# Delta-rule stage of a hybrid encoder layer: the remainder of weight pieces by a negated rounding and an adding DMA

## The chip, the cores and the metric

One core of one Trainium2 chip runs the whole program. The metric is the device time of one execution in microseconds. The engines are TensorE (PE; PEld is its weight load, which overlaps), VectorE (DVE), ScalarE (ACT), GpSimd (POOL) and SyncE (SP, which issues DMAs). Each engine works through its own instructions in order; semaphores join the engines.

## The reference

One encoder layer over 640 tokens (512 of a prompt, 8 x 16 of a decoding group), model width 2048, all in fp32. Cut to its core:

```
z = x @ w_in                     # one projection: attention, delta-rule and gate columns
y_a = (fox_attend(q_a, k_a, v_a, forget) * silu(gate_a)) @ w_out_fox
qkv = silu(causal_conv4(qkv_b)); q, k = l2_normalize(q), l2_normalize(k)
o_b, state = gated_delta_chunked(q, k, v, g, beta, state0)
y_b = (rms_norm(o_b) * silu(gate_b)) @ w_out_gdn
h = (sigmoid(m_a) * y_a + sigmoid(m_b) * y_b) @ w_out
x1 = layer_norm(alpha * x + h)
out = x1 + sigmoid(x1 @ w_pl_gate) * rms_norm(p @ w_pl_proj)
```

The keys, values, forget logits, the convolution's last rows and the delta-rule states are outputs too.

## The kernel before

**Products in three parts.** An fp32 product is made of fp32r ("rounded") operands: a weight w is split into wh, its rounded value, and wl = w - wh, an operand x likewise into xh and xl. TensorE adds wh·xh, wh·xl and wl·xh. The 640 tokens are cut into two halves of 320, so one step of 128 weight rows takes six matmuls of 320 columns (`mm6`, called from `column`, L380 and L381). A column of 128 outputs has 16 such steps.

**From memory to a piece.** The weights come as halves of 128 x 1024 into `wr`, three buffers, by SyncE's DMA (L266, 512 KB). A half is cut into two pieces of 512 columns, each of which serves four steps. For each piece `w_piece` issues two instructions: ScalarE casts it to `wh` (L326), and VectorE subtracts, `wl` = `wr` - `wh` (L327). `wh` and `wl` have five buffers each (`PIECES`), so a new piece may overwrite a buffer when TensorE has used the piece made five earlier. `w_ahead` is called once in each step, ahead of its matmuls; it may issue one load and make one piece, if fewer than five are outstanding.

**Stages.** The front and the attention fill the time to about 900 us. In the delta-rule stage (about 945 to 1645 us, `phase_gdn`) the columns are those of q, k, v and gate for eight heads, and merge-gate columns that fill in between. Then come the output projections and the tail. For a part of the later columns sums of weights are prepared on GpSimd (`weight_sums`, L292, tile `ws`) and kept in memory (`wsums`).

**Lanes.** Between the steps of a column `tick` (L124) lets generators ("lanes") issue their next small step: the convolution (`strip`, L836 to L843, and `conv_silu` with `tails`, L849), the block work of a head (L978 on), the chunks (`gdn_chunks`, L998; `gdn_dec`, L1052) and the heads' ends (L1022 to L1042). At the start of `gdn_chunks` GpSimd copies `kpad`, `gpad` (L1003) and `uu` (L1008); six ticks later the first decode matmuls (L1060) read `kpad`. In `gdn_dec` GpSimd makes `vm` from ScalarE's `vnd` (L1069, L1072). In the recurrence over tokens ScalarE makes `vn` (L1162) from one small matmul for the next (L1165). The last head's normalised output is transposed by TensorE (L1037, L1041), multiplied on VectorE and split (L354, L355) as operand 15 of the columns that follow.

**What sets the order.** The program writes the order of every engine out by itself. `saw` adds an estimated duration for each instruction to a clock for its engine (VectorE 0.17 us + 0.0011 per element of a row, ScalarE 0.21 + 0.00085, GpSimd 0.25 + 0.0020), and a lane's next step is issued once the estimated result is due. So an instruction that goes to another engine moves the lanes' steps against the columns. Within one queue nothing is passed.

Of the kernel before, what the change touches and what calls it, by code (L numbers as in the profile page):

```python
# [9 lines left out]
F32 = mybir.dt.float32  # L10
# [4 lines left out]
ALU = mybir.AluOpType  # L15
# [37 lines left out]
class Kernel:  # L53
# [143 lines left out]
    def plan(self):  # L197

        n = self.i["w"].shape[0] // 2
        self.ops, self.halves, c = [], [], 0
        self.short = range(n - 48 + self.PLAIN, n - 40)
        self.wsums, self.later = {}, [*self.short, *range(n - 32, n - 16, 2), *range(n - 16 + self.GATES, n, 2)]
        while c < n:
            if c in self.short:

                for x in ("S2", "b"):
                    self.wsums[c, x] = self.tc.dram_tile([P, 1024], F32, name=f"ws{c}{x}")
                for i, (x, p) in zip((0, 1, 4, 3, 2, 6, 5), ((0, 0), ("S2", 0), ("S2", 1), ("b", 0), (0, 1), ("b", 1), (1, 1))):  # L210
                    if p == 0 or x == 1:
                        self.halves.append((c, x, "wr", 1 if x == 1 else 2))
                    self.ops.append(("p", (c, x), p, ((c, i), 0)))
                c += 1
                continue
            if c in self.later:

                for x in ("S1", "S2", "b", "S3"):
                    self.wsums[c, x] = self.tc.dram_tile([P, 1024], F32, name=f"ws{c}{x}")
                for i, key in enumerate(((c, 0), (c, "S2"), (c, 1), (c, "b"), (c, "S1"), (c + 1, 1), (c, "S3"))):  # L220
                    self.halves.append((*key, "wr", 2))
                    self.ops += [("p", key, p, ((c, i), p)) for p in range(2)]
                c += 2
                continue
            if self.PAIR0 <= c < self.PAIR0 + self.PAIRS * 2:
                self.halves += [(c, 0, "wr", 4), (c + 1, 0, "wr", 4), (c + 1, 1, "sr", 3), (c, 1, "wr", 3)]
                o = [("p", (c, 0), 0),
                     ("s", (c, "S1"), (c + 1, 0), (c + 1, 1), ALU.add),
                     ("s", (c, "S2"), (c, "S1"), (c, 0), ALU.subtract),
                     ("p", (c, "S2"), 1),  # L230
                     ("s", (c + 1, 0), (c, 0), (c + 1, 0), ALU.subtract),
                     ("p", (c, 1), 2),
                     ("s", (c, "S2"), (c, 1), (c, "S2"), ALU.subtract),
                     ("p", (c + 1, 0), 3), ("p", (c, "S1"), 4), ("p", (c + 1, 1), 5), ("p", (c, "S2"), 6)]
                for x in o:
                    if x[0] == "s":
                        self.ops.append(x)
                    else:
                        self.ops += [("p", x[1], p, ((c, x[2]), p)) for p in range(2)]
                c += 2  # L240
                continue
            cs = range(c, c + (2 if c == 0 else 1))
            for p in range(4):
                for x in cs:
                    if p % 2 == 0:
                        self.halves.append((x, p // 2, "wr", 2))
                    self.ops.append(("p", (x, p // 2), p % 2, (x, p)))
            c += len(cs)
        self.raw, self.wq, self.used = {}, {}, 0
        self.rest = 0  # L250
        self.nh = self.no = self.np = 0

    def w_new(self, tag):
        pool = self.wp if tag == "wr" else self.zp
        return pool.tile([P, 1024], F32, tag=tag, name=tag, bufs=3)
# [62 lines left out]
    def w_piece(self):  # L318
        nc = self.nc
        _, key, p, to = self.ops[self.no]  # L320
        self.no += 1
        self.np += 1
        src = self.w_use(key)[:, p * 512:p * 512 + 512]
        hi = self.wp.tile([P, 512], F32R, tag="wh", name="wh", bufs=self.PIECES)
        lo = self.wp.tile([P, 512], F32R, tag="wl", name="wl", bufs=self.PIECES)
        nc.scalar.copy(out=hi, in_=src)  # L326
        nc.vector.tensor_tensor(out=lo, in0=src, in1=hi.bitcast(F32), op=ALU.subtract)  # L327
        self.wq[to] = (hi, lo)

    def w_ahead(self):  # L330

        if self.nh < len(self.halves) and self.now >= self.rest and self.w_free(self.halves[self.nh][2]):
            self.w_load()
        if self.no == len(self.ops):
            return
        o = self.ops[self.no]
        if o[0] == "s":
            if o[2] in self.raw and o[3] in self.raw and (o[1] in self.raw or self.w_free("sr")):
                self.no += 1
                self.w_sum(*o[1:])  # L340
        elif self.np - self.used < self.PIECES and o[1] in self.raw:
            self.w_piece()
# [90 lines left out]
    def pair(self, xf, fin, each=None, uv=None, half=False):  # L433
# [32 lines left out]
        def add(out, a, b):  # L466
            nc.vector.tensor_tensor(out=out, in0=a, in1=b, op=ALU.add)
        nc.scalar.copy(out=u, in_=run(0, "X11", "a"))
        w = body(u)
        add(w, w, run(1, "T2", "b"))  # L470
        if half:
            add(v, w, run(4, "T1", "c"))
# [712 lines left out]
    def run(self, ctx):  # L1185
        nc, tc = self.nc, self.tc
        nc.push_inst_callback(self.saw)
        ctx.callback(nc.pop_inst_callback)
        self.cst = ctx.enter_context(tc.tile_pool(name="cst", bufs=1))
        self.xp = ctx.enter_context(tc.tile_pool(name="xp", bufs=KT))  # L1190
        self.wp = ctx.enter_context(tc.tile_pool(name="wp", bufs=2))
        self.ps = ctx.enter_context(tc.tile_pool(name="ps", bufs=4, space=bass.MemoryType.PSUM))
        dr = tc.dram_tile
        self.ogd = [dr([P, T], F32, name=f"ogd{i}") for i in range(16)]
        self.md = [dr([P, T], F32, name=f"md{i}") for i in range(32)]
        self.ed = [dr([P, T], F32, name=f"ed{i}") for i in range(16)]
        self.ld = dr([5, 4, 32, 32], F32, name="ld")
        self.xd = dr([80, 256], F32, name="xd")
        self.sqd = dr([P, T], F32, name="sqd")
        self.es = [dr([P, T], F32, name=f"es{i}") for i in range(16)]  # L1200
        self.rr = [dr([P, T], F32, name=f"rr{i}") for i in range(16)]
        self.sgd = [dr([P, T], F32, name=f"sgd{i}") for i in range(H)]
        self.sgf = [dr([P, T], F32, name=f"sgf{i}") for i in range(H)]
        self.qkd = {(h, i): dr([P, T], F32, name=f"qkd{h}{i}") for h in (0, *self.APART) for i in range(2)}
        self.vd = dr([5, P, 1024], F32, name="vd")
        self.kc, self.vc, self.bias = {}, {}, {}
        self.plan()
        self.col = 0
        self.op = [None] * KT
        self.cut = slice(0, HALF), slice(HALF, T)  # L1210
        self.nm = 0
        work, conv, self.ends = self.lane(), self.lane(True), self.lane()
        self.blocks, self.chunks, self.sums = self.lane(True), self.lane(), self.lane(True)
        self.work = work
        with tc.manual_schedule():
            with tc.tile_pool(name="ps2f", bufs=3, space=bass.MemoryType.PSUM) as self.ps2:
                with tc.tile_pool(name="zs", bufs=1) as self.zp:
                    self.front(work)
                with tc.tile_pool(name="zf", bufs=1) as self.zp:
                    self.phase_fox(work)  # L1220
            with tc.tile_pool(name="ps2g", bufs=4, space=bass.MemoryType.PSUM) as self.ps2, \
                    tc.tile_pool(name="cs2", bufs=1) as c2, tc.tile_pool(name="zg", bufs=1) as self.zp:
                self.cvst = c2.tile([P, 24, 24], F32, name="cvst")
                nc.sync.dma_start(out=self.cvst, in_=self.i["conv"])
                self.tails = c2.tile([P, 24, 27], F32, name="tails")
                self.nbanks = 4
                self.phase_gdn(conv, work)
            with tc.tile_pool(name="ps2b", bufs=4, space=bass.MemoryType.PSUM) as self.ps2, \
                    tc.tile_pool(name="zb", bufs=1) as self.zp:
                self.tail()  # L1230
# [1211 lines left out]
```

## Time and profile before

| | us |
|---|---|
| median of 3 runs | 2189.33 (2188.91 to 2189.61) |
| span of the profiled execution | 2185.3 |
| outside the span (median less span) | 4.0 |
| PE busy in the span | 2168.4 (99%) |
| DVE busy | 1555.4 (71%) |
| ACT busy | 924.8 (42%) |
| POOL busy | 317.7 (15%) |
| casts to `wh` (L326), whole span | 638, 389.9 |
| subtractions to `wl` (L327), whole span | 638, 442.4 |

The profiled execution has no time of its own beside its span: what lies around the span is taken from the runs' median. Columns of a stretch ("windows") are explained where they are shown. In a group "x176 | 123.2, 701 | 112.0 <-ACT wh L326 110.3" says 176 instructions, 123.2 us busy, 701 ns each, and 112.0 us of idle time of their engine just before them, of which 110.3 were ended by ScalarE's `wh`. In a list of waits the three numbers are us in total, times, and the longest.

### The profile page before, as it was taken

How to read it: one execution, taken by the hardware profiler on the slowest of the kernel's cores; microseconds unless marked ns; L12 is line 12 of the kernel's file. 1: busy time of each engine (PE TensorE's matmuls, PEld its weight loads, DVE VectorE, ACT ScalarE, POOL GpSimd, SP SyncE). 2: the span in 40 equal slices, each digit the busy share in tenths (PEclk: the TensorE clock that was granted, in tenths of full speed). 3: DMA queues.
4: the chain of work that ended last, by engine and by line, in shares of the span. 5: the costliest groups of instructions: out<-in, count | busy, mean ns of one | idle time of the engine just before them, and what ended most of it. 6: DMA issues, size and time to landing. Idle time of an engine off the chain costs nothing. (4 is left out here: it accounts for less than half of the span.)

```text
span 2185.3 us, 41804 instructions
## 1 busy us (share of the span) xinstructions
PE 2168.4 (99%) x15606; PEld 2101.9 (96%) x15606; DVE 1555.4 (71%) x3194; ACT 924.8 (42%) x2058; POOL 317.7 (15%) x542
## 2 busy tenths in 40 slices
PE   9999999999999999999999999999999999999998
PEld 7799999999999999999999999999999999999998
DVE  6877677667455456676776867767757787789987
ACT  4344444444333345334434535435434343354544
POOL 0022323333111101111121211210000000011100
PEclk9999999999999999999999999999999999999999
DMA  6356665666888857844535444436567656673475
GB/s 233 104 183 198 201 190 185 196 198 212 319 293 282 303 190 246 289 115 132 151 115 148 133 117 145 135 116 190 174 213 256 220 168 205 195 270 137 149 229 172
DMA packets 222283, 421.12 MB, mean 193 GB/s; under 512 B 33768, under 2 KB 118840, under 8 KB 222080
## 3 DMA queue, kind: packets, MB, share of 16 engines
q1 hardware_dynamic: 222080, 418.45, 58.9%
q8 instruction: 123, 2.02, 0.4%
q14 instruction: 80, 0.66, 0.1%
HBM read 323.29 MB, written 95.07 MB: 191 GB/s over the span
## 5 line engine op out<-in xcount | busy, mean ns | idle before, releaser
L327 DVE TENSOR_TENSOR wl<-wr,wh 128x512 fp32r<-128x512 f32 x638 | 442.4, 703 | 287.6 <-ACT wh L326 281.4
L326 ACT CAST wh<-wr 128x512 fp32r<-128x512 f32 x638 | 389.9, 618 | 317.8 <-PE g L381 137.7
L380 PE MATMUL g<-xh,wh 128*128 128x320 f32 (+1 forms) x1184 | 385.1, 325 | 0.2 <-ACT xh L354 0.2
L380 PE MATMUL g<-xl,wh 128*128 128x320 f32 (+1 forms) x1184 | 366.0, 309 | 0.3 <-DVE xl L355 0.3
L381 PE MATMUL g<-xh,wh 128*128 128x320 f32 x1184 | 366.0, 309 | 0.0
L381 PE MATMUL g<-xl,wh 128*128 128x320 f32 x1184 | 365.7, 309 | 0.0
L380 PE MATMUL g<-xh,wl 128*128 128x320 f32 (+1 forms) x1184 | 365.7, 309 | 0.0
L381 PE MATMUL g<-xh,wl 128*128 128x320 f32 x1184 | 365.5, 309 | 0.0
L458 PE MATMUL g<-xh,wh 128*128 128x320 f32 (+1 forms) x1072 | 334.0, 312 | 2.3 <-ACT m L1241 1.6
L458 PE MATMUL g<-xl,wh 128*128 128x320 f32 (+1 forms) x1072 | 332.0, 310 | 0.6 <-DVE xl L355 0.6
L458 PE MATMUL g<-xh,wl 128*128 128x320 f32 (+1 forms) x1072 | 332.0, 310 | 0.0
L292 POOL TENSOR_TENSOR ws<-ws 128x171 f32<-128x171 f32 (+2 forms) x184 | 135.5, 736 | 771.9 <-DMA ws<-in_w 763.3
L380 PEld LDWEIGHTS g<-xh,wh 128*128 128x128 f32 x1184 | 223.0, 188 | 12.3 <-issue 8.0
L381 PEld LDWEIGHTS g<-xh,wh 128*128 128x128 f32 x1184 | 223.1, 188 | 0.9
L380 PEld LDWEIGHTS g<-xl,wh 128*128 128x128 f32 x1184 | 222.8, 188 | 0.9 <-DVE xl L355 0.9
L380 PEld LDWEIGHTS g<-xh,wl 128*128 128x128 f32 x1184 | 222.4, 188 | 0.2 <-DVE wl L327 0.2
L381 PEld LDWEIGHTS g<-xl,wh 128*128 128x128 f32 x1184 | 222.6, 188 | 0.0
L381 PEld LDWEIGHTS g<-xh,wl 128*128 128x128 f32 x1184 | 222.3, 188 | 0.0
L458 PE MATMUL g<-t,wh 128*128 128x320 f32 (+1 forms) x976 | 216.6, 310 | 0.0
L458 PEld LDWEIGHTS g<-xh,wh 128*128 128x128 f32 x1072 | 201.8, 188 | 4.1 <-ACT m L1241 2.1
L458 PEld LDWEIGHTS g<-xl,wh 128*128 128x128 f32 x1072 | 201.6, 188 | 1.2 <-DVE xl L355 1.1
L458 PEld LDWEIGHTS g<-xh,wl 128*128 128x128 f32 x1072 | 201.9, 188 | 0.0
(443 smaller groups left out, 3594.4 us busy)
## 6 DMA issues: line engine op xcount, KB each, us to landing
wr<-in_w SPq DMA_DIRECT2D x259, 512.0 KB, 4.1
kc<-in_kc SPq DMA_DIRECT2D x32, 512.0 KB, 6.4
vc<-in_vc SPq DMA_DIRECT2D x32, 512.0 KB, 6.9
ws<-in_w SPq DMA_DIRECT2D x96, 128.0 KB, 3.5
md<-m SPq DMA_DIRECT2D x32, 320.0 KB, 3.3
t<-md SPq DMA_DIRECT2D x32, 320.0 KB
sr<-in_w SPq DMA_DIRECT2D x18, 512.0 KB, 3.6
ws<-in_w SPq DMA_DIRECT2D x100, 85.5 KB, 2.5
```

The costliest lines, as they stand in the source:

```text
L292: nc.gpsimd.tensor_tensor(out=o, in0=x, in1=y, op=op)
L326: nc.scalar.copy(out=hi, in_=src)
L327: nc.vector.tensor_tensor(out=lo, in0=src, in1=hi.bitcast(F32), op=ALU.subtract)
L380: nc.tensor.matmul(ps[0], whl[w], xhl[o][:, a], start=(first and x == 0), stop=(last and x == 2))
L381: nc.tensor.matmul(ps[1], whl[w], xhl[o][:, b], start=(first and x == 0), stop=(last and x == 2))
L458: nc.tensor.matmul(ps, a[:, w], b, start=(k == 0 and n == 0 and not more), stop=(k == last and n == 2), skip_group_check=True)
```

## The change

For pieces that are made after the start of the delta-rule stage, of columns that are neither prepared sums nor among the last 48, the remainder is made in another way: ScalarE writes `lo` = -(the weights), which the fp32r tile rounds, so -wh; then a DMA on GpSimd's queue reads the same piece of the weights from memory and adds it to `lo` in place. The DMA is not issued in `w_piece`, but by `w_adds` in the first `w_ahead` that is at least one tick later. 160 of the 638 pieces are made so: all that belong to delta-rule heads and to merge gates in the stage.

```diff
--- before.py
+++ after.py
@@ -249,6 +249,8 @@
         self.raw, self.wq, self.used = {}, {}, 0
         self.rest = 0
         self.nh = self.no = self.np = 0
+        self.summed, self.adds = False, deque()
+        self.SUMMED = n - 48
 
     def w_new(self, tag):
         pool = self.wp if tag == "wr" else self.zp
@@ -324,11 +326,23 @@
         hi = self.wp.tile([P, 512], F32R, tag="wh", name="wh", bufs=self.PIECES)
         lo = self.wp.tile([P, 512], F32R, tag="wl", name="wl", bufs=self.PIECES)
         nc.scalar.copy(out=hi, in_=src)
-        nc.vector.tensor_tensor(out=lo, in0=src, in1=hi.bitcast(F32), op=ALU.subtract)
+        c, hf = key
+        if self.summed and key not in self.wsums and c < self.SUMMED:
+            nc.scalar.mul(lo, src, -1.0)
+            self.adds.append((self.now + 1, lo, self.i["w"][2 * c + hf][:, p * 512:p * 512 + 512]))
+        else:
+            nc.vector.tensor_tensor(out=lo, in0=src, in1=hi.bitcast(F32), op=ALU.subtract)
         self.wq[to] = (hi, lo)
 
+    def w_adds(self):
+
+        while self.adds and self.adds[0][0] <= self.now:
+            _, lo, src = self.adds.popleft()
+            self.nc.gpsimd.dma_start(out=lo, in_=src, accum_op=ALU.add)
+
     def w_ahead(self):
 
+        self.w_adds()
         if self.nh < len(self.halves) and self.now >= self.rest and self.w_free(self.halves[self.nh][2]):
             self.w_load()
         if self.no == len(self.ops):
@@ -1224,6 +1238,7 @@
                 nc.sync.dma_start(out=self.cvst, in_=self.i["conv"])
                 self.tails = c2.tile([P, 24, 27], F32, name="tails")
                 self.nbanks = 4
+                self.summed = True
                 self.phase_gdn(conv, work)
             with tc.tile_pool(name="ps2b", bufs=4, space=bass.MemoryType.PSUM) as self.ps2, \
                     tc.tile_pool(name="zb", bufs=1) as self.zp:
```

In the whole program this takes 160 instructions from VectorE (L327), adds 160 to ScalarE (L331) and 160 DMAs to GpSimd (L341, 256 KB each; GpSimd issued none before). SyncE's DMAs stay the same in number, and so do TensorE's matmuls: 13152 of the main stream (fp32r) and 1388 small ones (fp32). Their order changes: TensorE's row order passes 507 times from main matmuls to small ones or back before, 489 times now, so it leaves the main stream 9 times less. The planner counts the new instructions, and lane steps of the stage stand between 160 main matmuls earlier and 72 later than before. Outside the stage the order is the same. Lines shift: L326 is L328, the subtraction L334, and what stands behind is 14 lines further down (L1003 is L1017, L1037 is L1051).

On GpSimd's queue, at the start of a head's chunks in the middle of the stage; `ws` are the weight sums, `kpad`, `gpad` and `uu` the copies for the decode matmuls, `vm` the masked `vnd`. Before:

```order
L292 TENSOR_TENSOR ws<-ws 128x171 x8
L1003 COPY kpad<-kq_9936 128x4x16 x2
L1003 COPY gpad<-gr 128x4x16 x2
L1008 COPY uu<-u_11695 32x5x32 x4
L292 TENSOR_TENSOR ws<-ws 128x171 x4
L838 MEMSET strip 128x3
L843 COPY strip<-cvst 128x8x3
L849 COPY tails<-strip 128x3
L850 COPY tails<-strip 128x24
L1072 TENSOR_TENSOR vm<-vnd,cb 128x256
```

With the change:

```order
L341 DMA wl<-in_w 128x512 x5
L294 TENSOR_TENSOR ws<-ws 128x171 x4
L341 DMA wl<-in_w 128x512
L1017 COPY kpad<-kq_9936 128x4x16 x2
L1017 COPY gpad<-gr 128x4x16 x2
L1022 COPY uu<-u_11564 32x5x32 x4
L341 DMA wl<-in_w 128x512 x3
L1086 TENSOR_TENSOR vm<-vnd,cb 128x256
L341 DMA wl<-in_w 128x512
```

Adds (L341) now stand right in front of and behind the copies, and `vm` has three ahead of it and one behind.

On ScalarE's queue, around the convolution's copies out of PSUM in the same stage. Before:

```order
L1069 ACTIVATE vnd<-s,cs 128x128
L839 COPY strip<-g 128x320
L840 COPY strip<-g 128x192
L842 COPY strip<-g 128x8x16
L326 CAST wh<-wr 128x512
L854 ACTIVATE cy<-strip,taps 128x664
L1081 COPY ob<-s 128x128
L326 CAST wh<-wr 128x512
L1162 ACTIVATE vn<-s,cs 128x128
```

With the change:

```order
L328 CAST wh<-wr 128x512
L331 ACTIVATE wl<-wr 128x512
L853 COPY strip<-g 128x320
L854 COPY strip<-g 128x192
L856 COPY strip<-g 128x8x16
L328 CAST wh<-wr 128x512
L331 ACTIVATE wl<-wr 128x512
L868 ACTIVATE cy<-strip,taps 128x664
L1176 ACTIVATE vn<-s,cs 128x128
```

Each cast is followed by the scaling of the same piece (L331), which the lanes' own steps now have in front of them.

On TensorE's queue, at the last head's output transposes. Before, with 30 main matmuls (L458) between them and the first column of the next stage (L380):

```order
L458 MATMUL g<-xl,wh 128x320
L458 MATMUL g<-xh,wl 128x320
L1037 MATMUL s<-cb,ob 128x128 x4
L1041 MATMUL s<-cb,ob 128x128
L458 MATMUL g<-xh,wh 128x320
```

With the change:

```order
L472 MATMUL g<-xl,wh 128x320
L472 MATMUL g<-xh,wl 128x320
L1051 MATMUL s<-cb,ob 128x128 x4
L1055 MATMUL s<-cb,ob 128x128
L394 MATMUL g<-xh,wh 128x320
L395 MATMUL g<-xh,wh 128x320
```

The transposes have moved behind those 30 matmuls and stand directly ahead of the next stage's column.

## The prediction

> **What bounds the kernel now.** First the busy times by stretch (window; length; busy us and instructions of PE, PEld, DVE, ACT, POOL; granted clock; DMA share; GB/s). The change acts in the delta-rule stage, 945 to 1645 us.
>
> ```profile
> 945.00:1645.00 700.00, 697.86 (x5281) 673.69 (x5280) 500.53 (x1400) 303.78 (x843) 102.51 (x246) 1.00 0.49 147
> 300.00:400.00 100.00, 100.00 (x683) 100.00 (x683) 71.41 (x93) 40.65 (x77) 33.12 (x31) 1.00 0.59 189
> 546.00:765.00 219.00, 217.03 (x1840) 201.81 (x1840) 110.63 (x262) 77.28 (x195) 26.53 (x46) 1.00 0.86 299
> ```
>
> TensorE is idle for 700 − 697.86 = 2.14 us of the stage, at full clock. VectorE, which the change relieves, is busy 72% of it, ScalarE 43%, GpSimd 15%. The second row is a stretch of nothing but main matmuls: 100/683 = 0.1464 us each. Next, what TensorE waited for in the whole span (us in total, times, longest):
>
> ```profile
> PE g L458 <- ACT m L1241: 1.6, 1, 1.6
> ...
> PE s L1152 <- DVE S L1170: 1.2, 1, 1.2
> ...
> PE s L1165 <- ACT vn L1162: 0.8, 1, 0.8
> ...
> PE g L458 <- DVE wl L327: 0.2, 1, 0.2
> ```
>
> The subtraction that the change takes away (`wl`, L327) held TensorE up once in 2185 us, for 0.2 us. The 1.2 and the 0.8 are nearly all that was lost in the stage. So VectorE is no bound: the gain to be had is 2.14 us, plus whatever the new order saves in TensorE's own work. 0.2% of the time, about what a measurement can tell from no change, is 4.4 us.
>
> **The change part by part.** The groups of the stage (count | busy, mean ns | idle before, by releaser):
>
> ```profile
> L327 DVE TENSOR_TENSOR wl<-wr,wh 128x512 fp32r<-128x512 f32 x176 | 123.2, 701 | 112.0 <-ACT wh L326 110.3 <-DMA out_stp<-S 1.1
> L326 ACT CAST wh<-wr 128x512 fp32r<-128x512 f32 x177 | 109.9, 621 | 86.7 <-PE g L381 68.4 <-DMA wr<-in_w 10.4 <-PE g L458 3.2
> L292 POOL TENSOR_TENSOR ws<-ws 128x171 f32<-128x171 f32 x80 | 49.9, 624 | 101.6 <-DMA ws<-in_w 97.0
> L1008 POOL COPY uu<-u 32x160 f32<-32x160 f32 x32 | 12.4, 387 | 136.7 <-DMA u<-xd 80.8 <-PE g L381 54.9
> L1003 POOL COPY kpad<-kq 128x64 f32<-128x64 f32 x16 | 5.3, 359 | 0.0
> ```
>
> *Off VectorE:* 160 subtractions × 0.70 = 112 us, 500 to 389 of 700. Hidden before, so worth nothing by itself.
>
> *Onto ScalarE:* 160 scalings of the same 128x512 piece. No such instruction is in the trace; the cast L326, same engine and shape, takes 0.62, so +99 us, 304 to 403 of 700 (58%). It lies beside TensorE. What it may cost is lane steps (the delta rule's small matmuls) that wait behind a scaling on ScalarE's queue: nothing at the least, and at the most 0.62 in front of each of the four `vn` (L1162) of eight heads, 32 × 0.62 = 20 us. The program's planner counts ScalarE's time and sets those steps later, and in the whole stage ScalarE's `vn` cost 0.8; I take +0.7, that row once more.
>
> *Onto GpSimd:* 160 issues of an adding DMA, 256 KB each. GpSimd issued none before; the rows for an issue are SyncE's (min/median/max in ns of the weight loads, L266) and what these loads and others took to land:
>
> ```profile
> L266 SPq DMA_DIRECT2D wr<-in_w x82: 327/333/1519, 946.4 to 1644.5; - x82
> ...
> DMA to landing us min/median/max: 3.4/3.7/5.0
> ```
>
> ```profile
> wr<-in_w SPq DMA_DIRECT2D x259, 512.0 KB, 4.1
> ...
> ws<-in_w SPq DMA_DIRECT2D x100, 85.5 KB, 2.5
> ...
> es<-ed SPq DMA_DIRECT2D x16, 320.0 KB, 8.1
> ```
>
> An issue costs 0.33 to 1.5 us by these; I take 1.0, since GpSimd needs 0.36 even to copy 64 elements (L1003) where the bigger engines' cheapest work takes less. GpSimd goes from 102.5 to about 262 of 700. Landing: at least the 2.5 of an 85 KB load; at most 16.2, twice the slowest row, since an adding DMA reads its destination too. I take 4.1, the whole span's median for 512 KB: that is as many bytes as 256 KB read twice over, and the stage's DMA load moves towards the span's.
>
> Whether this is hidden is a budget. A piece is 24 matmuls, 24 × 0.1464 = 3.51 us; with five buffers a piece released is first needed after the four others, 14.06 us later, more where lane work stands between. One such release before, ScalarE and VectorE, with the last number the idle time ahead:
>
> ```profile
> 960.43 0.62 ACT L326 CAST wh<-wr 128x512 fp32r<-128x512 f32 x1 [2.90 <-PE g L381]
> ```
>
> ```profile
> 961.08 0.69 DVE L327 TENSOR_TENSOR wl<-wr,wh 128x512 fp32r<-128x512 f32 x1 [2.03 <-ACT wh L326]
> ```
>
> Before: cast and subtraction, 1.34 us of 14.06. Now: cast 0.62 + scaling 0.62 + up to four weight sums ahead on GpSimd 4 × 0.62 = 2.5 + issue 1.0 + landing 4.1 = 8.8. That leaves 5.2 us; cost nothing. If the cover is gone the price is steep: everything beyond 14.06 is shared out over five buffers, 0.2 us a piece for each us too late.
>
> *Waits added:* each add waits on GpSimd's queue for ScalarE's scaling (and for the add five pieces earlier, long landed). GpSimd used to run ahead; now it cannot pass TensorE's releases. Behind an add stand, at the start of each head, the copies `kpad`, `gpad` and `uu`, on which decode matmuls depend. They take 4 × 0.36 + 4 × 0.39 = 3.0 us and are issued six steps ahead, 6 × 6 × 0.1464 = 5.3 us: with one add of 1.0 in front 1.3 us are over; two take 0.3 of it back. I take 0 here; the rivals have the rest.
>
> *SyncE:* 160 subtractions no longer hold the raw weight buffer, but the scaling does, which ends as early (961.05 + 0.62 against 961.77). Loads come no later. Zero.
>
> *DMA traffic:* 160 × 256 KB = 41.9 MB more. By the page's queue row,
>
> ```profile
> q1 hardware_dynamic: 222080, 418.45, 58.9%
> ```
>
> 41.9 MB are 0.1 × 0.589 × 2185 = 129 us of all engines, or 258 with the destination read: the stage's share goes from 0.49 to 0.67 or 0.86. At 0.86 the third window above lost 1.97 of 219 us on TensorE; at that rate the stage would lose 6.3 instead of 2.14. So contention is worth 0 to +4.2; I take 0, as the waits of that window belong to work that the stage lacks.
>
> *Order:* the planner sees other engine times and places lane steps elsewhere. Counted over the order, TensorE now leaves the main stream 9 times less. What one such excursion costs beside its own matmuls:
>
> ```profile
> 1468.75 0.49 PE L1152 MATMUL s<-S,kq 128*128 128x128 f32 x2 [1.24 <-DVE S L1170]
> 1468.99 0.40 PE L380 MATMUL g<-xh,wh 128*128 128x320 f32 x1
> 1469.22 0.31 PE L381 MATMUL g<-xh,wh 128*128 128x320 f32 x1
> 1469.37 0.31 PE L380 MATMUL g<-xl,wh 128*128 128x320 f32 x1
> ```
>
> The first main matmul after it keeps TensorE 0.23 us, not 0.15: 9 × 0.08 = −0.75. The two waits of 1.2 and 0.8 are accidents of one placement and may go or come back elsewhere: −2.0 to 0, taken as −1.0. The last head's output transposes move to the very end of the stage, 30 matmuls or 4.4 us later. Their product was split for the next stage here:
>
> ```profile
> 1645.62 0.60 PE L1037 MATMUL s<-cb,ob 128*128 128x128 f32 x4
> ...
> 1655.44 0.81 DVE L355 TENSOR_TENSOR xl<-og,xh 128x640 fp32r<-128x640 f32 x1
> ```
>
> It is operand 15 of a column that starts 30 matmuls after 1646.1, at 1650.5, so due 15 × 0.88 = 13.2 later, at 1663.7. Ready at 1656.25, 7.4 to spare; 4.4 of it goes. Zero.
>
> **Sum:** 2185.3 − 1.0 − 0.75 + 0.7 = 2184.2 of span. The median of the runs, 2189.3, is 4.0 above the span; so 2188.3, −0.05%.
>
> **The rivals.**
>
> *Late landing (slower).* The add lands too late for five buffers. It decides from 14.06 − 0.62 − 0.62 − 1.0 = 11.8 us, or 9.3 with four weight sums ahead; say 10.5. For it: the row of 8.1 us for 320 KB, and that nothing in the trace reads its destination. Against: no load from the weights took over 5.0 in the stage. If 12 us: half of the 160 pieces (lanes shield the others, an assumption) × 1.5 × 0.2 = +24, so 2213; 16.2 would give +91.
>
> *GpSimd's queue (slower).* An issue takes so long that the head's copies come late: from 5.3 − 3.0 = 2.3 us. At 3.0 with one to two adds ahead, 0.7 to 3.7 late in each of 8 heads, 6 to 30 us, say +16: 2205. For it: these waits show how tightly GpSimd's other work follows ScalarE already,
>
> ```profile
> POOL tails L849 <- ACT strip L840: 139.9, 18, 14.0
> ...
> POOL vm L1072 <- ACT vnd L1069: 62.2, 7, 15.4
> ```
>
> so adds are caught behind them as well. Against: 1.5 is the slowest issue in the rows. A mechanism that would lengthen issues is VectorE working while GpSimd prepares a transfer: 389 us of VectorE's work stay, but those that copy or scale one fp32 operand out of SBUF are tiny.
>
> ```profile
> L188 DVE TENSOR_SCALAR rfy<-rft 128x5 int32<-128x5 int32 x8 | 1.5, 193 | 0.3
> ```
>
> The Trainium skill, "SBUF — State Buffer", section "Who interferes with whom", speaks against this change: a DMA issued from GpSimd stalls while VectorE runs an operation that takes both ports of the shared pair, about 620 ns becoming 3100. By it issues near 3.1 would be this rival; with such operations as short as the row above it would strike rarely, and no run here has shown it yet.
>
> *Faster by over 0.2%.* All of the stage's idle time gone, and the excursions: −2.14 − 0.75 = 2186.4, still within 0.2%. For 2184.9 or less TensorE would have to do its own matmuls faster, for which no row speaks.
>
> *It does not do what it says* I exclude: the order shows 160 subtractions gone and 160 adds there.
>
> **How the numbers follow.** No change 0.69 (its own range 2186.4 to 2193.5: idle time all gone; contention in full and a few ScalarE waits), late landing 0.14, GpSimd's queue 0.12, faster 0.05. Slower takes both rivals, 0.26. The range goes from 2186 to 2206: over the queue's price, below the landing's middle, which leaves out about 0.14 above and 0.04 below.
>
> **What would show it.** Right: TensorE idle for 1 to 3 us of the stage; the scaling near 0.62; adds landing in 3 to 6 us; no wait of TensorE on `wl`'s DMA. Late landing: waits of L380 on `wl<-in_w` in plain stretches, landing over 9. Queue: waits on `kpad`, `gpad`, `uu` or `vm`, GpSimd taking over 2 us from add to add. Contention: weight loads landing in 5 or more. If TensorE's main matmuls were spaced other than 0.146, the whole base of the sum would be wrong.

## The result and the profile after

The change made the kernel slower: 2207.8 us (median of 4 runs, 2205.3 to 2209.9) against 2189.5. The ratio is 1.0083, 95% interval 1.0071 to 1.0096, so +18.3 us where −1.0 was forecast, and just above the range's end of 2206.

Where it went shows in the busy times by stretch, with the same columns as before. (The DMA share adds up the times of the packets that start in a stretch, over 16 engines; it can come out a little above 1.) First the kernel before, at the stage's beginning, which the prediction's rows leave out:

```profile
870.00:945.00 75.00, 75.00 (x516) 74.88 (x515) 47.94 (x84) 29.67 (x76) 17.18 (x34) 1.00 0.77 251
```

Then the changed kernel, from there to the stage's end:

```profile
870.00:945.00 75.00, 65.93 (x422) 64.94 (x421) 28.00 (x57) 31.92 (x80) 21.80 (x36) 0.93 1.02 289
945.00:1020.00 75.00, 69.55 (x508) 68.42 (x507) 39.47 (x118) 38.03 (x93) 29.20 (x55) 0.98 0.87 201
1020.00:1600.00 580.00, 579.68 (x4375) 559.83 (x4374) 356.53 (x1078) 316.67 (x836) 184.01 (x338) 1.00 0.80 193
1600.00:1680.00 80.00, 77.81 (x596) 74.83 (x596) 45.07 (x100) 36.87 (x83) 2.37 (x5) 1.00 0.63 216
```

In 580 us, with most of the 160 adds, TensorE is idle for 0.32 us: there the change costs nothing, as forecast. The loss lies between 870 and 1020 us, with a little at the stage's end, and in the first two rows the granted clock is below 1 as well. TensorE's waits in the changed kernel, those that the kernel before did not have:

```profile
PE g L394 <- DMA wl<-in_w: 9.1, 3, 6.4
PE s L1125 <- DVE ss L938: 3.6, 1, 3.6
...
PE g L472 <- ACT ob L1046: 2.2, 1, 2.2
PE s L903 <- DVE kq L881: 1.9, 1, 1.9
```

They make 16.8 us; the two single waits before in the stage, 1.2 and 0.8, are gone. The parts of the change themselves in the changed kernel, 945 to 1665 us: scalings (L331), adds (L341, whose time on GpSimd is that of the issue; ns min/median/max) and the adds' landing.

```profile
L331 ACT ACTIVATE wl<-wr x138: 622/628/667, 947.2 to 1527.0; 128x512 fp32r<-128x512 f32 x138
L341 POOL DMA_DIRECT2D wl<-in_w x138: 850/862/890, 948.1 to 1527.9; - x138
...
DMA to landing us min/median/max: 3.6/5.5/9.8
```

**The wait of 6.4 us**, step by step: ScalarE, GpSimd and TensorE of the changed kernel around 900 us.

```profile
892.67 0.65 ACT L328 CAST wh<-wr 128x512 fp32r<-128x512 f32 x1
893.19 0.66 ACT L331 ACTIVATE wl<-wr 128x512 fp32r<-128x512 f32 x1
```

```profile
893.35 0.20 POOL L864 COPY tails<-strip 128x24 f32<-128x24 f32 x1
903.42 1.25 POOL L294 TENSOR_TENSOR ws<-ws 128x171 f32<-128x171 f32 x2 [9.87 <-DMA ws<-in_w]
904.70 0.88 POOL L341 DMA_DIRECT2D wl<-in_w  x1
```

```profile
913.11 0.64 PE L394 MATMUL g<-xh,wl 128*128 128x320 f32 x1 [6.42 <-DMA wl<-in_w]
913.54 0.47 PE L395 MATMUL g<-xh,wl 128*128 128x320 f32 x1
913.81 0.47 PE L394 MATMUL g<-xh,wh 128*128 128x320 f32 x1
...
919.52 0.31 PE L395 MATMUL g<-xl,wh 128*128 128x320 f32 x1
919.67 0.31 PE L394 MATMUL g<-xh,wl 128*128 128x320 f32 x1
```

The scaling ended at 893.9. Its add was issued only at 904.7, because GpSimd stood for 9.87 us at a weight sum that waited for its load. It landed 8.4 us later, at 913.1, and TensorE had stood for 6.4 us by then. Behind that, main matmuls start every 0.267 us in place of 0.147 until about 918. The prediction's own budget gives this wait: from the start of the cast to the landing the piece took 913.1 − 892.7 = 20.4 us, where 14.06 were to be had; 6.3 are missing, and TensorE stood for 6.4.

**The wait of 2.4 us**, which ended at 937.2, has no weight sum in front. Its add was issued at 927.8, 0.3 us after its scaling, and landed 9.4 us later. Here it was the cast that came late: TensorE wanted the piece at 934.8, so by the budget its buffers were free from about 934.8 − 14.06 = 920.7, and the cast began at 926.3. ScalarE and VectorE before it:

```profile
923.88 0.44 ACT L821 ACTIVATE sc<-g 128x320 f32<-128x320 f32 x1 [9.88 <-DVE sg L823]
...
926.29 0.65 ACT L328 CAST wh<-wr 128x512 fp32r<-128x512 f32 x1
```

```profile
921.95 0.89 DVE L842 SCALAR_TENSOR_TENSOR es<-es,plw,re 128x640 f32<-128x640 f32 x1 [3.42 <-DMA es<-ed]
```

ScalarE stood for 9.88 us at a gate's step (`sc`) that waited for VectorE, and VectorE stood in its own order at the rescaling of e, whose loads (`es<-ed`, 320 KB) landed in 13.6 us in the median between 865 and 925 us, against 8.1 before. So this wait comes from a slow landing and a cast that stood in order behind work that waits for a load, on other queues than GpSimd's.

For the rest I follow one number: how much later the n-th main matmul starts than the same one of the kernel before, worked out from all 12840 starts in both traces. The executions differ by 0.3 to 5 us before the stage begins, where nothing was changed but in the two rows with four buffers, so differences along a row count.

```
main matmul           4600   5400   6000   8200   8400   9000   9600  12800
start before, us     837.5  960.5 1062.8 1455.0 1491.0 1595.4 1693.3 2171.7
the change            +1.4  +15.1  +22.0  +22.7  +20.0  +17.7  +21.3  +21.3
adds after rescale    +1.0   +1.0   +0.8   +1.5   +1.0   -2.0   +4.9   +4.9
adds in rescale only  +1.4  +11.1  +10.9  +11.3  +11.3  +11.3  +11.3  +11.2
adds between          +1.1   +1.1   +0.9   +1.6   +1.6   +1.6   +1.0   +1.0
order of before       +0.3  +12.6  +12.6  +12.6  +16.4  +16.4  +15.8  +15.8
 and after rescale    +2.3   +2.3   +2.3   +2.3   +6.8   +6.8   +7.0   +7.2
 and sums later       +2.4   +4.1   +4.1   +4.1   +9.1  +10.8  +13.1  +13.1
weight sums later     +1.0   +3.9  +11.1  +11.8   +8.8  +15.0  +10.1  +10.4
slower rescaling      +1.5  +10.9  +10.0  +11.7  +11.2   +8.2  +15.4  +15.3
scaling only          +2.0   +2.0   +1.9   -0.2   +1.7   +2.0  +21.1  +21.4
four buffers          +3.7  +17.1  +17.7  +23.8  +22.5  +22.5  +28.3  +36.2
before, four buffers  +5.1   +5.1   +5.1   +5.1   +5.3   +5.3   +4.3   +9.9
```

The change's 19.9 us beyond the +1.4 fall at the stage's start (13.7), near 1000 us (6.9) and then, up and down with the moved lane steps, −0.7.

### The profile page after: what moved, and what is told of

Read it like the earlier page. It is cut to its first block, busy times and chain, and to the rows that moved or that the text cites. A ratio compares the mean times of both kernels' runs of the same rounds, so it can differ in the third digit from the quotient of the medians.

```text
span 2206.6 us, 42074 instructions
## 1 busy us (share of the span) xinstructions
PE 2174.0 (99%) x15606; PEld 2107.2 (95%) x15606; DVE 1461.4 (66%) x3034; ACT 1008.4 (46%) x2218; POOL 438.9 (20%) x702
## 3 DMA queue, kind: packets, MB, share of 16 engines
q1 hardware_dynamic: 222080, 418.45, 58.4%
q0 software_dynamic: 23040, 41.95, 11.4%
## 5 line engine op out<-in xcount | busy, mean ns | idle before, releaser
L328 ACT CAST wh<-wr 128x512 fp32r<-128x512 f32 x638 | 390.2, 619 | 300.9 <-PE g L395 122.8
L334 DVE TENSOR_TENSOR wl<-wr,wh 128x512 fp32r<-128x512 f32 x478 | 330.8, 704 | 175.6 <-ACT wh L328 170.0
L472 PE MATMUL g<-xh,wh 128*128 128x320 f32 (+1 forms) x1072 | 334.1, 312 | 4.3 <-ACT ob L1046 2.2
L472 PE MATMUL g<-xl,wh 128*128 128x320 f32 (+1 forms) x1072 | 332.0, 310 | 0.6 <-DVE xl L369 0.6
L472 PE MATMUL g<-xh,wl 128*128 128x320 f32 (+1 forms) x1072 | 332.0, 310 | 0.0
L394 PEld LDWEIGHTS g<-xh,wl 128*128 128x128 f32 x1184 | 223.6, 189 | 10.0 <-DMA wl<-in_w 9.9
L395 PEld LDWEIGHTS g<-xh,wl 128*128 128x128 f32 x1184 | 223.4, 189 | 0.0
L472 PE MATMUL g<-t,wh 128*128 128x320 f32 (+1 forms) x976 | 216.4, 310 | 0.0
L341 POOL DMA_DIRECT2D wl<-in_w x160 | 138.8, 871 | 347.9 <-ACT wl L331 289.0
L472 PEld LDWEIGHTS g<-xh,wh 128*128 128x128 f32 x1072 | 201.8, 188 | 6.0 <-ACT ob L1046 2.4
L472 PEld LDWEIGHTS g<-xl,wh 128*128 128x128 f32 x1072 | 201.6, 188 | 1.1 <-DVE xl L369 1.1
```

The source lines that it names most:

```text
L341: self.nc.gpsimd.dma_start(out=lo, in_=src, accum_op=ALU.add)
L394: nc.tensor.matmul(ps[0], whl[w], xhl[o][:, a], start=(first and x == 0), stop=(last and x == 2))
L395: nc.tensor.matmul(ps[1], whl[w], xhl[o][:, b], start=(first and x == 0), stop=(last and x == 2))
L472: nc.tensor.matmul(ps, a[:, w], b, start=(k == 0 and n == 0 and not more), stop=(k == last and n == 2), skip_group_check=True)
```

## The experiments

Theory A: the adds are hidden by the five buffers except at the stage's start, where they meet the rescaling of e. `scale_e` there loads and stores 16 tiles `es` of 320 KB, while the weight sums do their loads and stores too; when it is through it sets `self.scaled`, by which the experiments tell the two times apart. Of each edit only the lines that matter are shown. Rival B: 160 adds cost a little each, everywhere. Within A two mechanisms: A1, GpSimd's queue stands behind a weight sum that waits for its load; A2, the DMA engines are full and the adds land late by themselves.

### Adds only after the rescaling, and only in it

```diff
-        if self.summed and key not in self.wsums and c < self.SUMMED:
+        if self.summed and self.scaled and key not in self.wsums and c < self.SUMMED:
```

> Adds only once the rescaling of e (the 32 transfers of es of 320 KB at the start of the stage) is done; 141 of 160 adds left, the first 19 pieces are subtracted on VectorE as before. Theory A (adds collide with the start of the stage; later they are hidden): the two waits on wl, 6.4 and 2.4 us, and the slower matmuls behind them go; what TensorE loses near 1013 us (1.9 + 3.6 and slow matmuls, from a late gr<-rd) may stay: 2190 to 2197. Rival B (the cost is one of the adds everywhere, 160 times a little): 141/160 of +18 stays, about 2205.

Measured: 2193.27 us, ratio 1.0021 (1.0011 to 1.0030). No wait on `wl` is left and TensorE loses nothing to matmul 9000, with 141 adds. What remains is one wait at the end, on the last head's output:

```profile
PE s L1051 <- ACT ob L1046: 3.4, 1, 3.4
```

The reverse has `not self.scaled` in that condition:

> The reverse: only the pieces made before the rescaling of e is done get an add (17 of them), all later ones are subtracted on VectorE. Theory A: one wait of about 6 us on wl near 912 us, with the slow matmuls behind it, stays: 2196 to 2202. Rival B: 17/160 of +18, about 2191.

Measured: 2197.45, ratio 1.0039 (1.0025 to 1.0054). Seventeen adds cost 9.7 us between matmuls 4600 and 5400 and nothing else in the program moves. Its waits:

```profile
PE g L394 <- DMA wl<-in_w: 7.1, 3, 6.3
```

Rival B has fallen: 17 adds at the start cost more than 141 afterwards.

### The weight sums later

```diff
+        while self.summed and not self.scaled:
+            yield 2
         for c in self.later[pairs]:
```

> All 160 adds, but the weight sums of this stage (loads, GpSimd's additions, stores) start only after the rescaling of e. Theory A1 (the add of 904.7 us was issued 8 us late because GpSimd stood behind a weight sum that waited for its load): the wait of 6.4 goes, 2195 to 2201. Rival A2 (the DMA engines are full and the add lands late by itself): the es transfers are still there, the wait stays at 4 us or more, 2203 or more.

Measured: 2196.68, ratio 1.0037 (1.0025 to 1.0050). The same 60 us, the change first, then this experiment:

```profile
865.00:925.00 60.00, 53.30 (x348) 52.45 (x347) 27.22 (x38) 20.24 (x40) 18.19 (x34) 0.94 1.04 298
```

```profile
865.00:925.00 60.00, 60.00 (x411) 59.55 (x410) 25.69 (x35) 27.49 (x69) 14.71 (x25) 1.00 1.03 309
```

The DMA engines are as full (1.04 and 1.03) and the adds take as long to land there, median 7.4 us against 7.9 with the change; TensorE is busy all the 60 us. So full DMA engines and slow landings of the adds alone are hidden; the wait of 6.4 takes the hold on GpSimd in front. That is A1. It is shown less clearly for the wait of 2.4, which is gone too: with the sums later the loads of `es` landed in 9.6 us in the median and not in 13.6, so for that wait the two theories are not told apart. The wait near 1000 us stays (4.4 us, on the same `ss` as in the change).

### A slower rescaling

```diff
-            yield 2
+            yield 4
             nc.sync.dma_start(out=self.es[n], in_=e[n])
```

> All 160 adds and the weight sums as in the change, but the rescaling of e takes a step every four ticks instead of two, so its 32 transfers are spread over twice the time. A1: the weight sums' loads come in time at a DMA load nearer to 0.8, so the 6.4 goes as well, 2194 to 2202; A2: the same. Rival B: 2207, as the adds are as many.

Measured: 2201.97, ratio 1.0062 (1.0047 to 1.0077), at the edge of what was expected and not in the way expected. The DMA engines did not get emptier (1.03 against 1.02 in the change), and five waits on `wl` took the place of three:

```profile
870.00:945.00 75.00, 68.63 (x453) 67.49 (x452) 24.29 (x33) 30.36 (x63) 22.85 (x37) 0.98 1.03 285
```

```profile
PE g L394 <- DMA wl<-in_w: 7.0, 5, 3.7
PE s L1051 <- ACT ob L1046: 2.7, 1, 2.7
```

As an experiment it tells nothing between A1 and A2, since the DMA engines stayed full. Its longest wait, 3.7 us, ended with the landing of an add that GpSimd had issued behind weight sums after standing for 8.59 us for their loads, which is A1's picture again. The wait near 1013 us is gone here, with all adds made, so that one hangs on where lane steps stand.

### Adds in the middle of the stage only

```diff
         for h in range(H):
+            self.summed = h < 7
```

on top of the first experiment.

> As the first experiment (adds only after the rescaling of e), and no adds any more from the last head on, so that the last head's output transposes stand 30 matmuls ahead of the next stage's column again, as before the change. Theory: what was left of the cost there is the wait of 3.4 us on the last head's output and 10 slower matmuls (1.2 us) behind it: 2187.5 to 2190, equal to the kernel before. Rival (the adds that remain, over 100, cost a little each): 2192 to 2193.

Measured: 2188.92, ratio 1.0002 (0.9993 to 1.0012), with 113 adds. The 3.4 us at the end are gone with the last head's adds. So a hundred and thirteen subtractions fewer on VectorE, 79 us of its work, are worth nothing that can be measured, and the adds that replace them cost nothing either. This is the best version found, and it beats nothing.

### ScalarE's part alone

```diff
-            self.adds.append((self.now + 1, lo, self.i["w"][2 * c + hf][:, p * 512:p * 512 + 512]))
-        else:
-            nc.vector.tensor_tensor(out=lo, in0=src, in1=hi.bitcast(F32), op=ALU.subtract)
+        nc.vector.tensor_tensor(out=lo, in0=src, in1=hi.bitcast(F32), op=ALU.subtract)
```

> ScalarE's 160 scalings as in the change, but no adds: VectorE subtracts as before, over the scaled buffer. Shows the part of ScalarE by itself. Theory: ScalarE's load makes the last head late (wait of 2 to 3.5 us and slower matmuls behind it if it is over 2.2), and nothing on wl: 2189.5 to 2194. Rival (ScalarE is behind the 1013 us wait too): 2196 or more.

Measured: 2208.89, ratio 1.0089 (1.0074 to 1.0104). The theory's number was wrong by 15 us; the time lies in the rival's range, but not by its mechanism. At matmul 9000 the delay is what it was before the stage, +2.0, so the scalings themselves are hidden; there is no wait near 1013 us, against the rival. All of the loss, 19 us, comes between matmuls 9000 and 9600, at the end of the stage. The two longest waits there are

```profile
PE s L1049 <- ACT ob L1044: 5.8, 1, 5.8
...
PE g L470 <- ACT ob L1044: 2.1, 1, 2.1
```

Here the planner counts the scaling as well as the subtraction, and the last head's steps run past the columns that should cover them (read from the trace, not tried by itself). That its total is near the change's is chance: the places have nothing in common. As a probe of ScalarE it is spoilt by the order, which the next runs hold fixed.

### The order of before held fixed

```diff
+            b = list(self.busy)
             nc.scalar.mul(lo, src, -1.0)
+            b[0] = max(b[0], b[1], self.clock) + 0.17 + 0.0011 * 512
+            self.busy = b
```

and the planner's times restored around the add's issue too. TensorE's rows are then those of the kernel before, one for one; what differs is only what the pieces cost.

> All 160 scalings and adds, but the planner counts each piece as it did before (a subtraction on VectorE, nothing on ScalarE and GpSimd), so that TensorE's order is row for row that of the kernel before. Theory: the two late adds at the stage's start stay (6.4 + 2.4 + 0.3, and 29 slower matmuls, 3.4 us), the waits near 997 and 1013 us and the one on the last head's output go, since they come from lane steps moved against the columns: 2200 to 2203. Rival (the 1013 us wait comes from the adds' traffic alone): 2205 to 2208.

Measured: 2205.23, ratio 1.0076 (1.0059 to 1.0093). In the table this is the cleanest row: +12.4 in the start, nothing for 500 us, +3.8 near 1484, nothing else of size. The waits near 997 and 1013 and at the end are gone: those came from the moved order. The time lies in the rival's range, but the wait that the rival spoke of is not there; what lifts it above the theory's is the wait near 1484, which was not expected.

> Adds only after the rescaling of e, all of them to the end of the stage, and TensorE's order that of the kernel before. Theory (late adds at the start and moved lane steps are all there is): 2188 to 2190.5, as before. Rival (ScalarE's load makes the last head late whatever the order): 2191 to 2194.

Measured: 2193.55, ratio 1.0023 (1.0013 to 1.0033): the theory's number was wrong, and the rival's place too. The +4.6 are one place, the same as in the run before. SyncE, VectorE and TensorE there, in this run:

```profile
1462.72 0.79 SPq L989 DMA_DIRECT2D lanes<-ld  x1
```

```profile
1469.54 0.41 DVE L997 TENSOR_TENSOR sx<-eye,lanes 80x248 f32<-80x248 f32 x1 [5.91 <-DMA lanes<-ld]
...
1472.99 0.34 DVE L1189 SCALAR_TENSOR_TENSOR S<-S,gl,s 128x128 f32<-128x128 f32 x1
```

```profile
1473.38 0.80 PE L1171 MATMUL s<-S,kq 128*128 128x128 f32 x2 [3.99 <-DVE S L1189]
```

and in the kernel before:

```profile
1460.46 0.78 SPq L970 DMA_DIRECT2D lanes<-ld  x1
```

```profile
1464.90 0.41 DVE L978 TENSOR_TENSOR sx<-eye,lanes 80x248 f32<-80x248 f32 x1 [2.57 <-DMA lanes<-ld]
```

A load of 320 KB, issued at the same place (2.26 us later, as everything in this execution), was there after 6.8 us in place of 4.4. VectorE waits for it in order, and behind it stands the state update `S` on which TensorE waits: 4.0 us in place of 1.2. Some 15 matmuls behind it at half pace add 15 × 0.12 = 1.8: 2.8 + 1.8 = 4.6. The DMA share around it is 0.81 (1457 to 1472 us) against 0.44 (1455 to 1470 before). This is the prediction's contention term.

> All 160 scalings and adds and the order of the kernel before (TensorE's rows the same up to the last head), and the weight sums of this stage start only after the rescaling of e. Theory A1 (of the 12.4 us lost at the stage's start nearly all comes from GpSimd standing behind weight sums that wait for their loads): the loss there falls to 1 to 3 us, the 4.6 near 1480 us stays: 2193 to 2197. Rival A2 (full DMA engines alone make the adds late): 2202 to 2206.

This is the fixed order with the weight sums after the rescaling. Measured: 2200.63, ratio 1.0054 (1.0037 to 1.0071), above what was expected: the last head's steps, from 1518 us on, could not be held in place here, and some 4 us are lost among them. At the start, for which it was made, the loss is 1.7 us where it was 12.4, with the DMA share at 1.05 from 870 to 945 us. With the order the same there, A1 holds, with the reserve on the wait of 2.4 us made above.

### Four buffers instead of five

```diff
-    PIECES = 5
+    PIECES = 4
```

in the changed kernel and in the one before.

> The change with four buffers for wh and wl in place of five. Budget from release to first use 3 x 3.51 = 10.5 us instead of 14.06; the path is 0.62 + 0.62 + 0.87 + 5.5 landing = 7.6 in plain stretches, 10.1 with four weight sums ahead, 10 with a landing of 7.9 at the stage's start. If the budget is right: many short waits on wl at the start of the stage and a few later, 2215 to 2240. If the budget plays no part: 2206 to 2212.

> The kernel before with four buffers for wh and wl, as the control for the run above. 1.34 of 10.5 us are used: 2189 to 2191 by the budget.

Measured: 2224.59, ratio 1.0161 (1.0146 to 1.0176), and 2196.55, ratio 1.0031 (1.0021 to 1.0040). The control is slower than expected, but not in this stage: between matmuls 4600 and 9600 it is at +5.1 and +4.3, and its losses lie at the program's two ends. In the stage the change with four buffers loses 24.6 (3.7 to 28.3), with five 19.9; waits on `wl` are 12.4 us in place of 9.1, and spread out as the budget expects: six of them, none over 3.0, and two of them in the stage's middle (near 1185 and 1356 us), where five buffers had none. So the budget is of the right kind. That 3.5 us less of it cost no more is partly luck: GpSimd's hold near 905 us is 3.4 us long in this run and not 9.9, so the one large wait is missing here.

### What idling does to the clock

```diff
+        for _ in range({462: 15, 472: 16, 482: 17, 492: 18, 502: 19, 512: 20, 522: 21, 532: 22}.get(self.np, 0)):
+            nc.vector.tensor_tensor(out=lo, in0=src, in1=hi.bitcast(F32), op=ALU.subtract)
```

in the kernel before; the planner's times are restored around these lines, so the order stays.

> The kernel before, with the subtraction of eight pieces between about 1820 and 1960 us repeated 15 to 22 times more on VectorE, so that TensorE stands idle for times between 0 and 5 us eight times. Theory from the gaps seen so far (none of 2.19 us or less is followed by slower matmuls in the delta-rule stage, all of 2.38 or more are): 10 to 16 matmuls at 0.267 us in place of 0.147 behind each gap of more than about 2.3 us, none behind shorter ones. Rival: the number of slow matmuls grows with the gap from zero on.

The pieces chosen fell in the delta-rule stage, from 1357 us on, and seven of TensorE's idle times became 9 to 14.6 us, so the range aimed at was missed. One execution, 2290.4 us. TensorE after the longest:

```profile
1724.59 0.79 PE L1156 MATMUL s<-S,kq 128*128 128x128 f32 x2 [14.60 <-DVE S L1174]
1725.45 0.47 PE L462 MATMUL g<-xl,wh 128*128 128x320 f32 x1
1725.72 0.47 PE L462 MATMUL g<-xh,wl 128*128 128x320 f32 x1
...
1728.12 0.47 PE L462 MATMUL g<-xh,wl 128*128 128x320 f32 x1
```

```profile
1724.50:1728.50 4.00, 3.91 (x15) 3.91 (x16) 2.39 (x6) 0.62 (x1) 0.00 (x0) 0.50 0.75 215
```

Eleven matmuls at 0.267 us, with a granted clock of 0.50, after 14.6 us of idling; 16 after the 6.4 us of the change; 12 after 2.4 us. The number does not grow with the idle time, so this rival falls. The theory's border near 2.3 us falls as well: an idle time of 1.8 us in this run, and one of 2.1 in the run with ScalarE's part alone, were followed by 11 and 12 slow matmuls, one of 2.9 in the change with four buffers by none.

## Why the prediction was wrong

**What held.** VectorE's relief was worth nothing. The scaling took 0.63 (0.62 forecast), the issue 0.86 (1.0), both hidden where the order stood still. In the long middle of the stage the budget held with a landing of 5.5 in place of 4.1: TensorE idle for 0.32 of 580 us. No add there was issued more than 2.7 us after the end of its scaling, close to the 2.5 that the sum allowed for. (The landing is counted from the start of the issue, so the issue stood in the sum twice; that made the budget tighter, not looser.) The DMA share came out at 0.80 between the two values given (0.67 and 0.86), and a byte of the adds kept the engines about twice as long as another one:

```profile
q1 hardware_dynamic: 222080, 418.45, 58.4%
q0 software_dynamic: 23040, 41.95, 11.4%
```

(11.4/41.95 against 58.4/418.45 per MB: 1.95.) The gain from the order's two vanished waits, 2.05, and from fewer excursions, 0.75 by the estimate, fits the −0.7 behind matmul 6000, with the 2.2 at the end against it, but was not tried by itself.

**What failed first: the budget's term "four weight sums ahead, 4 × 0.62 = 2.5".** It took the sums at their work and left out their waiting, though the quoted group row had it: 101.6 us idle before 80 of them, 97.0 on their loads. An add inherits that wait, 9.87 us in the case that cost the 6.4: 10.9 us from the end of the scaling to the issue, where the sum had 2.5. And the budget was drawn up for 945 to 1645 us, while the adds begin at 856, in a stretch with the DMA share at 0.77 before and 1.02 after, where landings take 7.9. Full engines without the hold are nearly hidden (the weight sums later, at the order of before: 1.7 us lost); with the hold they cost 12.4 us. A hold of such a length beside free DMA engines did not occur, since it is itself a wait for a load; with the middle's landing of 5.5 it would by estimate still have been 3.4 us too late (20.4 − 8.4 + 5.5 − 14.06).

**Contention, "0 to +4.2, I take 0".** With the order fixed it was 3.8 to 5.0 in three runs, the slower clock behind the wait included: one load that landed 2.4 us later, where VectorE's queue and then TensorE stood behind it. The sign named for it, weight loads landing in 5 us or more, came in the change itself (5.1 in the median, 3.7 before) and cost nothing in the stage's middle. I had argued from the whole window's loss; what mattered was a single load with no slack, and the kernel before showed it as its longest wait of the stage, the 1.2 on `S`.

**"The last head's transposes: zero".** I asked when their product is needed, and there was room. But they themselves have to wait for what they transpose: 3.4 us with adds after the rescaling, 2.7 with the slower rescaling. What is *made* late matters as well as what is *needed*. The 2.2 us of the change itself are another wait beside it: a main matmul (L472), twelve ahead of the transposes, which then waited for nothing. The profile puts it down to `ob`, which this matmul does not read. It waits for VectorE too, where `fx` (L481), the step that takes a finished product out of its bank, ended at 1669.8, just before it; it stood behind the small steps of the last head's scale, 1666.4 to 1669.4. This is read from the trace and was not tried by itself.

**The moved order near 1000 us.** VectorE stood 9.5 us for one load, and TensorE behind it, in the changed kernel:

```profile
1011.21 1.40 DVE L930 SCALAR_TENSOR_TENSOR dt<-gr,colT,cb 128x128 f32<-128x128 f32 x5 [9.52 <-DMA gr<-rd]
```

```profile
1012.98 0.44 PE L1125 MATMUL s<-m,lt 32*32 32x32 f32 x16 [3.59 <-DVE ss L938]
```

That load was issued at 1002.4 behind a store for which SyncE had waited 11.7 us. With the order of before there is no such wait under the same adds; the planner, which knows nothing of DMA, had moved the steps to where the loads came too late. The sum had no term for it. That it is SyncE's queue and not another part of the order was read from this trace and not tried by itself.

**No term for the clock.** The change has some 40 matmuls at half pace, 40 × 0.12 = 4.8 us, in three places, behind waits of 6.4, 2.4 and 3.6.

**The rivals.** GpSimd's queue, at 2205, came nearest, but not by its mechanism: an add's issue took 0.85 to 0.89 us in the stage and at most 1.19 at its start, where adds follow each other, and TensorE never waited for one of GpSimd's copies. The rule that speaks of VectorE locking GpSimd out ("SBUF — State Buffer", "Who interferes with whom", in the Trainium skill) did not show: 138 issues lie between 850 and 890 ns beside a VectorE that is 61% busy in the stage's middle. With the operations that it speaks of as short as in the prediction's row, 193 ns, this is no test of the rule. (The two figures that the prediction gives with it, 620 and 3100 ns, stand in that page's section "A bandwidth-pool intuition that's wrong (but worth ruling out)".) Late landing, as a mechanism of plain stretches, did not happen at a median of 5.5 against the 9.3 from which it was to decide.

## What to carry to other kernels

A job moved to a queue inherits all that its neighbours there wait for; the budget for it needs their waits, not their busy times, and has to be drawn up for the worst stretch in which the job runs, not for the stage's mean. An engine that is 72% busy beside one that is 99.7% busy is no target, and all that its relief can do is to move other work about, which here cost more than it saved. Where a planner sets the order, hold its costs fixed once: that splits what an edit costs from what the new order costs.

## What was not expected of the hardware

**Short idling halves TensorE's clock for a few microseconds.** Over the 14 profiles of this case, each idle time of 3.4 us or more (18 of them, up to 14.6) was followed by main matmuls at 0.267 in place of 0.147 us, 9 to 17 of them (6 and 8 in two cases where small matmuls came first). Of those between 1.4 and 3.0 us some were and some were not, and none under 1.4 that stood alone was. So such an idle time costs about 1 to 2 us more than it shows (9 to 17 times 0.12). The Trainium skill, "TensorE: Matmul & The Clock Gate", section "What's actually happening", tells of a window of about 3.4 us that runs freely and of a clock that is either full or half. The traces agree on the two clocks: the granted clock was 0.50. That times between 1.4 and 3.0 go either way would fit a window whose place is not fixed, but then a window cannot have to be idle from end to end; no run here shows how it decides. Its rule of no gaps over about 3.4 us (section "HAM oscillation — how this bites in real kernels") is too generous here, since 2.4 us was enough in the change.

**An adding DMA from GpSimd** of 128 x 512 fp32 costs 0.86 us of issue on GpSimd (up to 1.19 in the change where adds follow each other), 3.6 to 9.8 us to land (5.5 in the median at a DMA share of 0.80, 7.9 at 1.04), and about twice (1.95 times) the DMA time per byte of the other transfers.
